# x first on SyncE's ring, all weights on ScalarE's, and sixteen small marks: a streamed x @ W kernel on one core

## Chip, cores and metric

One core of one Trainium2 chip. The metric is the device time of one execution in microseconds (us); the median of several. Each experiment is compared with runs of the kernel before on the same chip, beside it; a run over 1.5% above the fastest of its kernel is called slow and is left out of comparisons. Engines: TensorE (PE, its weight loads PEld), VectorE (DVE), ScalarE (ACT), GpSimd (POOL), SyncE (SP). "ACTq" and "SPq" in a profile are the queues of the two engines that issue DMAs here. I call what each feeds its ring; both rings run on the same 16 DMA engines.

## The reference

```python
W_adapted = W + scale * (lora_A @ lora_B)            # 256 x 256, rank 16
W_norm = np.sqrt(np.sum(W_adapted ** 2, axis=0, keepdims=True) + 1e-8)
W_final = W_adapted / W_norm * m
y = x.reshape(-1, 256) @ W_final                     # x: 32768 x 256, float32
```

32 MB of x come in, 32 MB of y go out; the weights are 256 KB of W, 16 KB each of lora_A and lora_B, 1 KB of m.

## The kernel before

x is cut into 8 blocks of 4 MB (128 rows of 32 KB, one per partition; the last block in two halves). There are five buffers. SyncE sends the first five loads at once; load b (b >= 5) waits until the store of block b - 5 has landed, since y overwrites x in the buffer and the buffer is then filled again.

```python
def load_x(n):
    nc.sync.dma_start(out=in_sbuf(*parts[n]), in_=in_dram(x_flat, *parts[n])
    ).then_inc(sem(f"load{n}"), 16)
def store_y(n):
    nc.scalar.dma_start(out=in_dram(out_flat, *parts[n]), in_=in_sbuf(*parts[n])
    ).then_inc(sem(f"store{n}"), 16)

nc.sync.dma_start(out=w_nat[:], in_=W...).then_inc(sem("load_w"), 16)
nc.scalar.dma_start(out=a_nat[:], in_=lora_A...).then_inc(sem("load_a"), 16)
nc.scalar.dma_start(out=b_nat[:], in_=lora_B).then_inc(sem("load_b"), 16)
nc.scalar.dma_start(out=m_row[:], in_=m[None, :]).then_inc(sem("load_m"), 16)
for n in range(len(parts)):
    b = parts[n][0] // CH
    if b >= XBUFS and parts[n][0] % CH == 0:
        nc.sync.wait_ge(sem(f"store{b - XBUFS}"), 16)
    load_x(n)
...
# VectorE, the end of the weights' chain
nc.vector.reciprocal(out=rnorm[:], in_=norm[:]).then_inc(dv, 1)
nc.vector.wait_ge(dv, 7)
for t in range(KC):
    i = nc.vector.tensor_mul(out=w_final[:, t], in0=wam[:, t], in1=rnorm[:])
i.then_inc(dv, 1)
...
# GpSimd: x to bf16 pairs, two chunks at a time, as soon as a block has landed
for p in range(NPR):
    ...
    nc.gpsimd.tensor_copy(out=xb_bufs[p % NXB][:], in_=x_bufs[...]).then_inc(sem("rounded"), 1)
...
# TensorE, in order: the weights' chain, then per pair of chunks transposes and products
nc.tensor.wait_ge(dv, 8)
...
# ScalarE: PSUM back into the x buffer; after each block drain(), then store_y(n)
```

Of the kernel before, what the change touches and what calls it, by code (L numbers as in the profile page):

```python
# [11 lines left out]
def kernel(  # L12
# [10 lines left out]
    nc = tc.nc  # L23
    P = 128
    FP32 = mybir.dt.float32
# [9 lines left out]
    KC = IN // P  # L35
# [7 lines left out]
    XBUFS = 5  # L43
    CH = DJ // J
# [15 lines left out]
    def sb(name, shape, dtype):  # L60
        return ctx.enter_context(nc.sbuf_tensor(name, shape, dtype))
# [7 lines left out]
    w_nat = sb("w_nat", [P, KC, OUT], FP32)  # L69
# [13 lines left out]
    norm = sb("norm", [P, OUT], FP32)  # L83
    rnorm = sb("rnorm", [P, OUT], FP32)
    m_all = sb("m_all", [P, OUT], FP32)
    w_final = sb("w_final", [P, KC, OUT], BF16)

    xt_ps = [ps(f"xt_ps{k}", [P, F8], FP32) for k in range(2)]
# [11 lines left out]
    def sem(name):  # L100
        if name not in sems:
            sems[name] = tc.alloc_semaphore(name)
        return sems[name]
# [4 lines left out]
    parts = [(b * CH, CH) for b in range(NBLK - 1)]  # L108
# [6 lines left out]
    def in_sbuf(g0, cnt):  # L115
        b, c = divmod(g0, CH)
        return x_bufs[b % XBUFS][:, c * J : (c + cnt) * J, :]

    def in_dram(dram, g0, cnt):
        return dram[g0 * J * P : (g0 + cnt) * J * P].rearrange("(p j) k -> p j k", p=P)  # L120

    def load_x(n):
        nc.sync.dma_start(
            out=in_sbuf(*parts[n]), in_=in_dram(x_flat, *parts[n])
        ).then_inc(sem(f"load{n}"), 16)

    def store_y(n):
# [2 lines left out]
        ).then_inc(sem(f"store{n}"), 16)  # L130


    nc.sync.dma_start(
        out=w_nat[:], in_=W.rearrange("(p t) o -> p t o", t=KC)
    ).then_inc(sem("load_w"), 16)
    nc.scalar.dma_start(
        out=a_nat[:], in_=lora_A.rearrange("(p t) r -> p t r", t=KC)
    ).then_inc(sem("load_a"), 16)
    nc.scalar.dma_start(out=b_nat[:], in_=lora_B).then_inc(sem("load_b"), 16)
    nc.scalar.dma_start(out=m_row[:], in_=m[None, :]).then_inc(sem("load_m"), 16)  # L140
    for n in range(len(parts)):
        b = parts[n][0] // CH
        if b >= XBUFS and parts[n][0] % CH == 0:
            nc.sync.wait_ge(sem(f"store{b - XBUFS}"), 16)
        load_x(n)


    nc.gpsimd.memset(zeros[:], 0.0).then_inc(sem("pool"), 1)
# [2 lines left out]
        out=identity[:],  # L151
        in_=zeros[:],
# [6 lines left out]
    for p in range(NPR):  # L159
        b, c = divmod(p, PRB)  # L160
        if p == 0 or part_of[2 * p - 1] != part_of[2 * p]:
            nc.gpsimd.wait_ge(sem(f"load{part_of[2 * p]}"), 16)
        if p >= NXB:
            nc.gpsimd.wait_ge(sem("turned"), p - NXB + 1)
        nc.gpsimd.tensor_copy(  # L165
            out=xb_bufs[p % NXB][:],
            in_=x_bufs[b % XBUFS][:, 2 * c * J : 2 * (c + 1) * J, :],
# [16 lines left out]
        out=wa[:], in0=ab_ps, scalar=float(scale), in1=w_nat[:], op0=ALU.mult, op1=ALU.add  # L184
# [15 lines left out]
    for p in range(NPR):  # L200
        nc.vector.wait_ge(sem("turned"), p + 1)
        nc.vector.tensor_copy(  # L202
            out=xt_bufs[p % NXT][:].rearrange("p r t -> p (r t)").bitcast(FP32),
            in_=xt_ps[p % 2][:],
# [8 lines left out]
        out=norm[:], in_=n2_ps, func=AF.Sqrt, bias=eps_col[:]  # L213
    ).then_inc(sem("act"), 1)
    for g in range(NCH):
        b, c = divmod(g, CH)
# [3 lines left out]
            out=x_bufs[b % XBUFS][:, c * J : (c + 1) * J, :], in_=y_ps[g % 2][:]  # L220
        ).then_inc(sem("room"), 1)
        n = part_of[g]
# [116 lines left out]
```

## Time and profile before

| | before |
|---|---|
| time, median of 3 runs | 163.86 us (163.66 to 163.94) |
| span of the profiled execution | 163.2 us (this run took 164.71; unprofiled runs of the same kernel beside e1 have spans of 162.1 to 162.6) |
| first store issued / sixth load may be sent (first store landed) | 34.5 us / 60.6 us |
| GpSimd's last wait for x ends; last store issued | 137.2 us; 148.2 us |

The profile's slices, the queues, SyncE's waits and the timeline of the start stand in the prediction. One more line of the groups matters later (count | busy us, mean ns of one | idle before): two multiplications of 128x256 took 2 us each, while another pair of the same shape (`wam`) took 0.42 us each.

```profile
L198 DVE TENSOR_TENSOR w_final<-wam,rnorm 128x256 bf16<-128x256 f32 x2 | 4.0, 2028 | 0.0
```

The trace also holds every DMA packet (its ring, size, start and duration, not its engine). Numbers called "packet records" come from there; their clock was set against the timeline by the landing of the first load, to about 0.1 us.

### The profile page before, as it was taken

Reading aid. Unit: us, or ns where it says so; the run is one execution under the profiler, and the core shown is the slowest. Engines: PE = TensorE matmul, PEld = TensorE weight load, DVE = VectorE, ACT = ScalarE, POOL = GpSimd, SP = SyncE. Lnnn points to the kernel's source line nnn. Section 1 sums busy time; section 2 is a strip of 40 time slices with the busy share of each in tenths; the row PEclk is TensorE's granted clock in tenths of the full one; section 3 lists DMA queues with packets and bytes.
Section 4 is the critical chain, followed back from the end, with each engine's and each line's share of the span. In section 5 each row is a group of like instructions: output and inputs, shape, how many; then the busy total and the mean of one; then the engine's idle time right before and its main releaser. Section 6 shows DMA issues by size and latency. Waiting matters only on the chain. (4 is left out here: it accounts for less than half of the span.)

```text
span 163.2 us, 1988 instructions
## 1 busy us (share of the span) xinstructions
PE 105.3 (65%) x786; PEld 85.2 (52%) x786; DVE 47.2 (29%) x44; ACT 63.8 (39%) x67; POOL 62.5 (38%) x39
## 2 busy tenths in 40 slices
PE   1270599789789897898981998619988820892000
PEld 0130577677577775776760867418676610771000
DVE  0429452350532514405230325005051400330000
ACT  3010027548366384473754053900738440062000
POOL 1006381753935738268004940069209003900000
PEclk9999999999999999999998589985899996599755
DMA  5998998998999999999999999999999999998991
GB/s 201 402 498 386 426 474 385 482 418 265 466 426 426 442 410 466 426 394 482 418 426 442 420 426 458 402 458 410 446 414 454 414 446 422 450 442 377 442 430 60
DMA packets 2915, 67.41 MB, mean 413 GB/s; under 512 B 465, under 2 KB 482, under 8 KB 610
## 3 DMA queue, kind: packets, MB, share of 16 engines
q1 hardware_dynamic: 1440, 33.82, 49.0%
q10 hardware_dynamic: 1474, 33.59, 47.8%
q14 instruction: 1, 0.01, 0.0%
HBM read 33.85 MB, written 33.55 MB: 413 GB/s over the span
## 5 line engine op out<-in xcount | busy, mean ns | idle before, releaser
L219 ACT COPY x_sb<-y_ps 128x1024 f32<-128x1024 f32 x64 | 61.9, 1014 | 75.8 <-PE y_ps L281 75.8
L165 POOL CAST xb<-x_sb 128x2048 bf16<-128x2048 f32 x32 | 60.0, 1902 | 79.3 <-DMA x_sb<-in_x_dram 56.0
L281 PE MATMUL y_ps<-w_final,xt 128*128 128x256 bf16 x512 | 64.6, 280 | 12.8 <-PEq L256 12.8
L202 DVE COPY xt<-xt_ps 128x1024 f32<-128x1024 f32 x32 | 38.2, 1221 | 88.1 <-PE xt_ps L267 88.0
L281 PEld LDWEIGHTS y_ps<-w_final,xt 128*128 128x128 bf16 x512 | 48.4, 100 | 28.2 <-issue 19.8
L267 PE MATMUL xt_ps<-identity,xb 128*128 128x128 f32 x264 | 39.1, 309 | 23.1 <-PEq L256 23.1
L267 PEld LDWEIGHTS xt_ps<-identity,xb 128*128 128x128 f32 x264 | 34.9, 161 | 25.8 <-issue 25.6
L198 DVE TENSOR_TENSOR w_final<-wam,rnorm 128x256 bf16<-128x256 f32 x2 | 4.0, 2028 | 0.0
L244 PE MATMUL y_ps<-sq,ones 128*128 128x256 f32 x4 | 2.1, 674 | 1.6 <-DVE sq L187 1.6
L233 PE MATMUL y_ps<-identity,a_nat 128*16 128x128 f32 x2 | 0.6, 397 | 3.6 <-DMA a_nat<-in_lora_A_dram 3.6
L212 ACT ACTIVATE norm<-y_ps,eps_col 128x256 f32<-128x256 f32 x1 | 0.5, 473 | 6.1 <-PE y_ps L244 6.1
L244 PEld LDWEIGHTS y_ps<-sq,ones 128*128 128x128 f32 x4 | 1.2, 323 | 2.3 <-DVE sq L187 2.1
L210 ACT ACT_TABLE_LOAD x1 | 1.3, 1283 | 2.4 <-issue 2.4
L233 PEld LDWEIGHTS y_ps<-identity,a_nat 128*16 128x16 f32 x2 | 0.1, 90 | 3.6 <-issue 3.6
L171 POOL MEMSET xb<- 128x2048 bf16 x1 | 1.8, 1805 | 0.3 <-PE xt_ps L267 0.3
L195 DVE RECIPROCAL rnorm<-norm 128x256 f32<-128x256 f32 x1 | 1.7, 1745 | 0.0
L237 PE MATMUL y_ps<-b_bf,aT 16*128 16x256 bf16 x2 | 0.6, 404 | 1.5 <-DVE aT L180 1.5
L189 DVE COPY m_all<-y_ps 128x256 f32<-128x256 f32 x1 | 0.4, 425 | 3.3 <-PE y_ps L249 3.3
L178 DVE CAST b_bf<-b_nat 16x256 bf16<-16x256 f32 x1 | 0.3, 281 | 3.8 <-DMA b_nat<-in_lora_B_dram 3.8
L249 PE MATMUL y_ps<-m_row,ones 1*128 1x256 f32 x2 | 1.2, 710 | 0.0
L237 PEld LDWEIGHTS y_ps<-b_bf,aT 16*128 16x128 bf16 x2 | 0.1, 106 | 1.9 <-DVE aT L180 1.9
L183 DVE SCALAR_TENSOR_TENSOR wa<-y_ps,w_nat 128x512 f32<-128x512 f32 x1 | 0.7, 692 | 0.8 <-PE y_ps L237 0.8
(13 smaller groups left out, 3.7 us busy)
## 6 DMA issues: line engine op xcount, KB each, us to landing
x_sb<-in_x_dram SPq DMA_DIRECT2D x7, 4096.0 KB, 27.1
out_dram<-x_sb ACTq DMA_DIRECT2D x7, 4096.0 KB, 37.2
x_sb<-in_x_dram SPq DMA_DIRECT2D x2, 2048.0 KB, 29.6
out_dram<-x_sb ACTq DMA_DIRECT2D x2, 2048.0 KB, 20.2
w_nat<-in_W_dram SPq DMA_DIRECT2D x1, 256.0 KB, 2.9
a_nat<-in_lora_A_dram ACTq DMA_DIRECT2D x1, 16.0 KB, 2.6
b_nat<-in_lora_B_dram ACTq DMA_DIRECT2D x1, 16.0 KB, 3.6
m_row<-in_m_dram ACTq DMA_DIRECT2D x1, 1.0 KB
```

The costliest lines, as they stand in the source:

```text
L165: nc.gpsimd.tensor_copy(out=xb_bufs[p % NXB][:], in_=x_bufs[b % XBUFS][:, 2 * c * J : 2 * (c + 1) * J, :],).then_inc(sem("rounded"), 1)
L171: nc.gpsimd.memset(xb_bufs[NPR % NXB][:], 0.0).then_inc(sem("rounded"), 1)
L183: nc.vector.scalar_tensor_tensor(out=wa[:], in0=ab_ps, scalar=float(scale), in1=w_nat[:], op0=ALU.mult, op1=ALU.add).then_inc(dv, 1)
L195: nc.vector.reciprocal(out=rnorm[:], in_=norm[:]).then_inc(dv, 1)
L198: i = nc.vector.tensor_mul(out=w_final[:, t], in0=wam[:, t], in1=rnorm[:])
L202: nc.vector.tensor_copy(out=xt_bufs[p % NXT][:].rearrange("p r t -> p (r t)").bitcast(FP32), in_=xt_ps[p % 2][:],).then_inc(sem("copied"), 1)
L210: nc.scalar.activation(out=warm[:], in_=eps_col[:], func=AF.Sqrt)
L219: nc.scalar.copy(out=x_bufs[b % XBUFS][:, c * J : (c + 1) * J, :], in_=y_ps[g % 2][:]).then_inc(sem("room"), 1)
L244: i = nc.tensor.matmul(n2_ps, ones[:], sq[:, t, :], start=(t == 0), stop=(t == KC - 1))
L249: nc.tensor.matmul(mb_ps, ones[0:1, :], m_row[:], start=True, stop=True).then_inc(pe, 1)
L267: i = nc.tensor.transpose(xt_ps[p % 2][:, j * P : (j + 1) * P], xb_bufs[p % NXB][:, j, :].bitcast(FP32), identity[:],)
L281: i = nc.tensor.matmul(y_ps[h][:, j, :], xt_bufs[p % NXT][:, r : r + P, t], w_final[:, t, :], start=(t == 0 and (j % (J // 2)) == 0), stop ...
```

## The change

Intent: x, the long stream, should not stand behind W; so all weights go to ScalarE's ring. Sixteen loads of 1 to 16 rows, with row lengths of 68 to 128 bytes, are put behind the fifth load so that they can be told apart in the trace.

```diff
-    nc.sync.dma_start(
-        out=w_nat[:], in_=W.rearrange("(p t) o -> p t o", t=KC)
-    ).then_inc(sem("load_w"), 16)
     nc.scalar.dma_start(out=a_nat[:], ...
+    nc.scalar.dma_start(
+        out=w_nat[:], in_=W.rearrange("(p t) o -> p t o", t=KC)
+    ).then_inc(sem("load_w"), 16)
     nc.scalar.dma_start(out=b_nat[:], ...
     nc.scalar.dma_start(out=m_row[:], ...
     for n in range(len(parts)):
         b = parts[n][0] // CH
+        if b == XBUFS and parts[n][0] % CH == 0:
+            for k in range(1, 17):
+                nc.sync.dma_start(
+                    out=marks[0:k, k, 0 : 16 + k], in_=lora_B[0:k, 0 : 16 + k]
+                ).then_inc(sem("marks"), 16)
         if b >= XBUFS and parts[n][0] % CH == 0:
             nc.sync.wait_ge(sem(f"store{b - XBUFS}"), 16)
         load_x(n)
+    nc.sync.wait_ge(sem("marks"), 256)
```

More of the change, by code (lines that the diff above doesn't have):

```diff
@@ L85 @@
     m_all = sb("m_all", [P, OUT], FP32)
+    marks = sb("marks", [16, 17, 32], FP32)
     w_final = sb("w_final", [P, KC, OUT], BF16)
```

## The prediction

> **What bounds the kernel now.** I read the slices of the span first, then the queues, then the waits, then the timeline of the start.
>
> ```profile
> DMA  5998998998999999999999999999999999998991
> GB/s 201 402 498 386 426 474 385 482 418 265 466 426 426 442 410 466 426 394 482 418 426 442 420 426 458 402 458 410 446 414 454 414 446 422 450 442 377 442 430 60
> ...
> q1 hardware_dynamic: 1440, 33.82, 49.0%
> q10 hardware_dynamic: 1474, 33.59, 47.8%
> HBM read 33.85 MB, written 33.55 MB: 413 GB/s over the span
> ```
>
> The DMA engines are busy in every slice; the two rings (q1 is SyncE's, q10 ScalarE's) together take 96.8% of 16 engines' span. No compute engine passes 65%, and the chain of work that ended last is only 145 to 148 us: what follows is stores draining. So the time is one start (first packet at 2.45 us) plus the packets of 67.4 MB plus whatever the DMA engines stand idle. In the trace's packet records each 4 MB load or store is 128 rows of 32 KB, 8 per DMA engine, and the median row takes 1.213 us on either ring; 8 blocks in and out are 128 rows per engine, 128 x 1.213 = 155.3 us. With the start and some 2 us of small packets and stalls, most engines end near 160 us; one ends at 163.2. Only something that makes DMA engines idle can cost much here, and only removed idle time can gain.
>
> ```profile
> SPq L123 <- DMA out_dram<-x_sb: 95.5, 3, 56.8
> ...
> POOL xb L165 <- DMA x_sb<-in_x_dram: 56.0, 6, 12.2
> ```
>
> There are five buffers: SyncE sends five loads at once, then waits 56.8 us for the first store to land before it may send the sixth. Until then the SyncE ring holds 40 rows per engine, 40 x 1.213 = 48.5 us of work, and no more. If the stores start after these have run out, nothing is left to move. When they start is set by the weights:
>
> ```profile
> 0.90 0.40 ACTq L136 DMA_DIRECT2D a_nat<-in_lora_A_dram  x1
> 0.94 0.37 SPq L133 DMA_DIRECT2D w_nat<-in_W_dram  x1
> ...
> 1.33 0.45 ACTq L139 DMA_DIRECT2D b_nat<-in_lora_B_dram  x1
> 1.36 2.39 SPq L123 DMA_DIRECT2D x_sb<-in_x_dram  x5
> ...
> 5.00 0.28 DVE L178 CAST b_bf<-b_nat 16x256 bf16<-16x256 f32 x1 [3.79 <-DMA b_nat<-in_lora_B_dram]
> ...
> 14.05 3.98 DVE L198 TENSOR_TENSOR w_final<-wam,rnorm 128x256 bf16<-128x256 f32 x2
> 18.30 3.27 PEld L267 LDWEIGHTS xt_ps<-identity,xb 128*128 128x128 f32 x16 [7.92 <-issue]
> ...
> 34.52 0.37 ACTq L128 DMA_DIRECT2D out_dram<-x_sb  x1
> ```
>
> lora_B lands at 4.95 us, the chain from it to w_final ends at 18.03, TensorE only then begins on x (in order), and the first store is issued at 34.52: 29.6 us after lora_B. Later stores follow each 13.2 us (47.74, 60.96, 74.22, 87.43), less than the 2 x 9.7 us that a block's load and store take, so compute has slack. With five loads sent at 1.4 us the loads alone would end near 52 us; the first store comes 18 us before that. This slack hides the weights today.
>
> **What the Trainium skill says.** "DMA: Bandwidth & Descriptors", section "Issuing engines are not separate DMA queues": DMAs of all issuers end on the same 16 engines and interleave. The trace agrees: both rings are busy together at an unchanged sum near 430 GB/s. Same page, "Queues, rings and completion order": an engine round-robins between rings and drains a whole packet, typically 9 to 17 descriptors, before it switches. The trace fits a turn of one descriptor better. m's single 1 KB row came at 6.30 us and its semaphore write at 7.55, one 32 KB row between them. And from 3.2 to 3.5 us, while lora_A (8 rows of 128 bytes per engine) and W (8 of 2 KB) were both in the rings, 40 packets of the one and 52 of the other started, mixed; lora_A packets went on until 3.5 us, which a whole group of 8 at 13 ns each would not. Same page, "Why a DMA increments its semaphore by 16 and not by 1": k of the 16 engines take part, the lowest-numbered, with k from the outer sizes. The trace shows one data packet for m and 16 for lora_B. So of marks with 1 to 16 rows, engine 0 gets 16 and engine 15 one.
>
> **The change part by part.** Compute is untouched but for line numbers; the comparison of the two orders moves only DMA issues.
>
> (a) x goes first on SyncE's ring: W's issue (0.42 us) leaves the way, and its 8 x 84 ns = 0.67 us per engine are moved, not saved. DMA starts at 2.45 us either way. Gain: none, as bytes bind.
>
> (b) The weights all stand on ScalarE's ring, against x rows of 1.213 us instead of each other. Per engine: lora_A 8 packets and a semaphore write, W 8 and one, lora_B one and one: 20 turns. Before, in the first 0.1 us of packets 27 of lora_A's 128 had started and 5 of W's, so the slowest engine gets perhaps one or none out ahead: 19 to 20 turns, each behind one record of SyncE's ring. 19 to 20 such records are 17 or 18 rows and 2 semaphore writes. 17.5 x 1.213 = 21.2, plus W's 0.67, plus a first row that takes some 0.3 longer (1.35 to 1.69 us in the trace), after 2.5: lora_B lands at 24.7 us, 19.7 later than now. W lands about one row earlier, m two turns later, in time for its matmul 4.9 us after lora_B.
>
> (c) The first store moves from 34.52 to 34.52 + 19.7 = 54.2 us. The five loads end at 2.5 + 0.3 + 48.6 + 0.8 (weights) = 52.2. The DMA engines then stand. Before, the first store's rows came 5.55 us after its issue (40.07), of which up to 1.2 was a running x row, and x rows were slowed to 2 to 2.9 us meanwhile (the slice of 265 GB/s; 1.5 us lost per engine). I take 3.0 us from issue to flow: 1.5 as at the start of the kernel (issue at 0.94, packet at 2.45) and this 1.5. Flow at 57.2, so 5.0 us idle.
>
> (d) The first store alone takes 9.7 us, to 66.9; the second is issued at 54.2 + 13.2 = 67.4 and flows at 68.9; the sixth load, sent on the first store's landing, flows at 66.9 + 1.5 = 68.4. Idle 1.5 us. After that ten blocks are left, 97 us, with a load and a store in hand at each step: block 4 is computed to 107 us, load 5 lands near 88. Nothing starves.
>
> (e) The marks: 16 data and 16 semaphore packets on engine 0, 2 on engine 15, near 10 ns each. They come after the fifth load, when by (c) the other ring is empty: under 1 us, in idle time. SyncE's issue of 16 x 0.4 us ends at 10 us while its ring is full.
>
> Sum: 5.0 + 1.5 idle, less the 1.5 us that the stall cost before and that (c) counts again, = +5.0. 163.86 + 5.0 = 168.9 us.
>
> **Rivals.** First: turns are whole packets, as the skill says. Then lora_B takes 6 turns, lands near 10 us, the first store goes at 39.6, 12 us before the loads run out: no idle, 163.5 to 164.3. For it: the page; against: m and the mixture above.
>
> Second, following from the first: if stores flow when the marks come up, each of engine 0's 32 mark packets waits behind a 1.21 us store row, up to 39 us, and the sixth load on engine 0 lands near 105 instead of 86.5. Compute then stalls at block 5. But the engine moves stores meanwhile, and the last store would be issued near 150 with backlog left: 163.5 to 168.
>
> Third: the slack of compute vanishes. TensorE would run without the pauses of 8 to 11 us that it has now from 88 us on; the granted clock already falls to 0.84 in 90 to 110 us. If blocks then take 16 us, the last store is issued near 157, still under the 166 at which the rows end; slower yet gives up to 172.
>
> Fourth: the author's hope, x first by 0.4 us and all else hidden: 163.4.
>
> **Range and chances.** Turns of one descriptor I hold to be 80% likely; then 165.5 to 171.5, as lora_B's landing and the store's start-up each are good to 1.5 us and count one for one. Otherwise near 164. Range 163.6 to 171.5. The line of 2% is 167.14, 1.8 us under my figure: slower 0.70, same 0.27, faster 0.03.
>
> **What would show it.** lora_B landing at 23 to 26 us (about 10 in the first rival); w_final ending near 37.7; first store issued at 53 to 56; one or two slices of low GB/s between 52 and 70 us; SyncE's first wait for a store longer than 56.8 us by some 8; no pause of GpSimd for x at the sixth block; the total bytes unchanged. Wrong if the slices stay at 9 throughout, or if the sixth load lands late on engine 0 alone. If lora_B is late as said and the time still within 2%, then the idle gap was mis-sized: the store's start-up of 3 us or the 17.5 rows.

## The result

The changed kernel takes 165.63 us in the median (165.49, 165.62, 165.64, and one slow run of 169.02); the kernel before, beside it, 163.9. The ratio is 1.0104 (95% interval 1.0085 to 1.0124). Ratios here are the mean time of one kernel's fast runs over that of the other's of the same rounds, so not quite the ratio of the medians. The forecast was +5.0 us; measured is +1.7, a third of it.

The slices of the changed kernel, to set beside those in the prediction: no slice of low DMA share between 52 and 70 us, where I had expected the engines to stand.

```profile
DMA  5999999999999899999989999999999999999992
GB/s 187 457 408 416 428 472 392 472 424 392 488 400 384 384 472 370 384 440 448 384 384 464 432 400 480 402 428 412 444 444 436 408 476 400 464 424 400 428 444 88
```

The timeline of the changed kernel (start us, duration, engine and line; in brackets the idle time before and who ended it):

```profile
0.90 0.40 ACTq L135 DMA_DIRECT2D a_nat<-in_lora_A_dram  x1
0.94 2.66 SPq L124 DMA_DIRECT2D x_sb<-in_x_dram  x5
...
1.33 0.45 ACTq L138 DMA_DIRECT2D w_nat<-in_W_dram  x1
1.81 0.45 ACTq L141 DMA_DIRECT2D b_nat<-in_lora_B_dram  x1
...
13.75 3.73 POOL L174 CAST xb<-x_sb 128x2048 bf16<-128x2048 f32 x2 [12.07 <-DMA x_sb<-in_x_dram]
21.54 0.28 DVE L187 CAST b_bf<-b_nat 16x256 bf16<-16x256 f32 x1 [20.32 <-DMA b_nat<-in_lora_B_dram]
...
30.59 0.76 DVE L207 TENSOR_TENSOR w_final<-wam,rnorm 128x256 bf16<-128x256 f32 x2
31.62 3.28 PEld L276 LDWEIGHTS xt_ps<-identity,xb 128*128 128x128 f32 x16 [4.71 <-issue]
...
47.37 0.37 ACTq L129 DMA_DIRECT2D out_dram<-x_sb  x1
...
63.36 39.38 SPq L124 DMA_DIRECT2D x_sb<-in_x_dram  x4
```

lora_B is there at 21.5 us (4.95 before; 24.7 forecast). W lands 17.6 us after its issue instead of 2.9. The two multiplications to w_final take 0.76 us together instead of 3.98; GpSimd's first casts are long over (e12 and other runs below show that this is the reason). The first store is issued at 47.37 us: 12.9 later than before, not 19.7. SyncE waits 53.1 us for it. That is less than the 56.8 of before only because the issues of the marks keep SyncE busy until 10.3 us, so that the wait begins later; the store lands at 63.3 us, 2.8 later than before (60.55):

```profile
SPq L124 <- DMA out_dram<-x_sb: 90.9, 3, 53.1
```

In the packet records the first store's rows flow from 51.8 us and the last row of the five loads ends at 54.6. The rows of the store came 2.8 us before the loads ran out, so the DMA engines never stood. But SyncE's ring, which before always had the sixth load queued behind the fifth, was without x rows from 54.6 to 68.0 us: 8.7 us until the store had landed, and 4.6 more from the issue of the sixth load (63.36) to its first row. (The sixth load of before began no earlier, at 68.4, but behind the fifth without a break.) The records differ in their slow rows. Summing over all rows what each took beyond 1.213 us (0.611 for a row of 16 KB), per DMA engine:

| stretch, us | before | changed |
|---|---|---|
| 0 to 5 (first rows of x) | 0.1 | 0.6 |
| 34 to 55 (first store's start) | 1.3 | 0.7 |
| 55 to 70 (sixth load's and second store's start) | 0.0 | 0.8 |
| 70 to 90 (third store's start) | 0.0 | 0.6 |
| whole execution | 1.65 | 2.95 |
| landing of the last store's 16 parts: mean, latest | 160.4, 163.2 | 161.5, 163.9 |

So 1.3 us more of DMA time per engine are lost in rows that take 1.4 to 2.4 us instead of 1.2: 0.5 more in the first 5 us, 0.6 less at the first store, 1.4 more between 55 and 90 us. The first part goes with x first, not with the gap: the kernels below that send x first in whole blocks have 0.5 to 0.7 us there, with a gap or without, those with W first 0.1. The later slow rows are mostly rows of the other ring in the last 1 to 5 us before a ring's rows begin again: SyncE's at 49 to 52 us, before the first store's rows (51.8); ScalarE's at 62 to 68, before the sixth load's (68.0); SyncE's at 76 to 81, around the start of the third store's (79.7). (The profiled run of before was 0.8 us slower than its neighbours. Two later kernels with the same start and typical spans of 162.2 us, e4 and e5 below, have 1.1 to 1.2 us of slow rows, and their last stores land at 159.8 and 160.1 in the mean, 162.2 and 162.1 at the latest; against them the changed kernel has 1.8 us more of slow rows and ends 1.4 to 1.7 us later in the mean, 1.7 to 1.8 at the latest, which is about the measured difference.)

### The profile page after: what moved, and what is told of

Same layout as the page of the kernel before. It is cut to its first block, busy times and chain, and to the rows that moved or that the text cites. A ratio compares the mean times of both kernels' runs of the same rounds, so it can differ in the third digit from the quotient of the medians.

```text
span 164.0 us, 2005 instructions
## 1 busy us (share of the span) xinstructions
PE 99.6 (61%) x786; PEld 81.5 (50%) x786; DVE 43.8 (27%) x44; ACT 63.6 (39%) x67; POOL 62.3 (38%) x39
## 3 DMA queue, kind: packets, MB, share of 16 engines
q10 hardware_dynamic: 1618, 33.85, 48.5%
## 5 line engine op out<-in xcount | busy, mean ns | idle before, releaser
L228 ACT COPY x_sb<-y_ps 128x1024 f32<-128x1024 f32 x64 | 61.7, 1014 | 60.8 <-PE y_ps L290 60.8
L290 PE MATMUL y_ps<-w_final,xt 128*128 128x256 bf16 x512 | 62.7, 275 | 14.1 <-PEq L265 14.1
L290 PEld LDWEIGHTS y_ps<-w_final,xt 128*128 128x128 bf16 x512 | 47.4, 98 | 28.6 <-issue 21.0
L276 PE MATMUL xt_ps<-identity,xb 128*128 128x128 f32 x264 | 35.4, 291 | 12.4 <-PEq L265 12.4
L276 PEld LDWEIGHTS xt_ps<-identity,xb 128*128 128x128 f32 x264 | 32.2, 151 | 14.0 <-issue 13.8
L258 PEld LDWEIGHTS y_ps<-m_row,ones 1*128 1x128 f32 x2 | 0.5, 308 | 0.7 <-issue 0.7
## 6 DMA issues: line engine op xcount, KB each, us to landing
w_nat<-in_W_dram ACTq DMA_DIRECT2D x1, 256.0 KB, 17.6
b_nat<-in_lora_B_dram ACTq DMA_DIRECT2D x1, 16.0 KB, 19.7
```

The costliest lines, as they stand in the source:

```text
L228: nc.scalar.copy(out=x_bufs[b % XBUFS][:, c * J : (c + 1) * J, :], in_=y_ps[g % 2][:]).then_inc(sem("room"), 1)
L258: nc.tensor.matmul(mb_ps, ones[0:1, :], m_row[:], start=True, stop=True).then_inc(pe, 1)
L276: i = nc.tensor.transpose(xt_ps[p % 2][:, j * P : (j + 1) * P], xb_bufs[p % NXB][:, j, :].bitcast(FP32), identity[:],)
L290: i = nc.tensor.matmul(y_ps[h][:, j, :], xt_bufs[p % NXT][:, r : r + P, t], w_final[:, t, :], start=(t == 0 and (j % (J // 2)) == 0), stop ...
```

## The experiments

Two theories after the result. A: the late weights leave SyncE's ring empty, because the sixth load must wait for a late first store; bytes flow on, but each new start costs slow rows. B: the marks cost the time, by turns against store rows. A third thing had to be checked: whether the terms of my sum were as I read them (one turn per descriptor; the idle gap if the store is late enough; the cast beside the multiplications).

**e1: no marks.**

```diff
 (changed kernel)
-        if b == XBUFS and ...: sixteen mark loads
-    nc.sync.wait_ge(sem("marks"), 256)
```

> The changed kernel without its sixteen marks. Theory A (late weights make rings run empty, and each new start of a ring costs the DMA engines 0.6 to 0.8 us): nothing changes, 165.4 to 165.8 us, lora_B lands near 21.5 us, first store issued near 47.4. Theory B (the marks cost the time, by turns against store rows): back to 163.7 to 164.2 us.

Measured: runs of 164.46, 165.25 (fast), and 167.24, 167.49, 167.71, 168.35 (slow); before beside it 163.7. The reported verdict is unclear (ratio 1.0194, which is more than the two fast runs by themselves give: their mean is 1.007 times the 163.7). The profiled fast run has lora_B at 21.5, 3.0 us of slow rows and a mean landing of the last store's parts at 161.5, as in the changed kernel, but its latest part lands at 163.1 instead of 163.9. So without the marks the slow rows and the late end are still there: B as the whole cause is refuted in the trace. The times are too scattered to give the fast part better than +0.8 to +1.6 us, and do not exclude that the marks cost some tenths. Why two thirds of the runs fell in a slower state, I have no profile to say; their granted clocks (0.941 to 0.944) lie between those of the two fast runs (0.932 and 0.950).

**e2: marks only.** The kernel before, with the sixteen mark loads and the wait for them.

```diff
 (kernel before)
+        if b == XBUFS and ...: sixteen mark loads
+    nc.sync.wait_ge(sem("marks"), 256)
```

> The kernel before plus the sixteen marks, weights as before. Theory A: 163.7 to 164.4 us; the marks come up while stores flow (from 67 us), take a turn against a 1.21 us row each, and the sixth load lands late (100 to 107 us instead of 87.7) on the engines with most marks, but bytes still bind. Theory B: 165 us or more.

Measured: fast runs 167.65, 167.94, 168.90, ratio 1.0286 (1.0253 to 1.0318), slower. My theory A expected no cost and missed; B's figure came true in a kernel in which B's cause really acts. GpSimd's timeline and the slices:

```profile
113.78 3.73 POOL L173 CAST xb<-x_sb 128x2048 bf16<-128x2048 f32 x2 [35.85 <-DMA x_sb<-in_x_dram]
```

```profile
DMA  5999989899999999999999999999999799098997
GB/s 197 450 434 403 482 379 497 387 387 371 450 418 418 450 411 466 419 435 419 403 466 419 444 426 403 426 415 454 422 415 430 336 387 497 8 505 379 399 422 316
```

The sixth block arrives at 113.8 us instead of 87.8. This is the second rival of the prediction: the marks come up at 68 us while stores flow. In the packet records the 16 rows of the last mark (128 bytes) start one after another at 68.5, 71.0, 72.8, 75.2, 77.8 ... 99.9, 104.2: an engine with one mark more takes 2.4 us more in the mean (104.2 - 68.5, over 15), two turns (data and semaphore write) of one store row each. The one with all sixteen begins the sixth load near 106 us instead of 69. Compute starves, the stores run out, and the DMA engines stand, most of all in the slice of digit 0 and 8 GB/s (141 to 145 us): 4.4 us idle per engine in all. I had written that bytes would still bind; they did not. In the changed kernel the same marks began to take turns at 55 us, but the first store had been alone on the other ring and ended at 62.7; the remaining marks all passed between 62.7 and 63.5. The late weights protected it.

**e3: W in two loads**, nine turns more on ScalarE's ring.

```diff
 (changed kernel)
-    nc.scalar.dma_start(out=w_nat[:], in_=W...)
+    for t in range(KC):
+        nc.scalar.dma_start(out=w_nat[:, t, :], in_=W...[:, t, :]).then_inc(sem("load_w"), 16)
...
-nc.vector.wait_ge(sem("load_w"), 16)
+nc.vector.wait_ge(sem("load_w"), 32)
```

> The changed kernel with W loaded as two DMAs of 8 rows of 1 KB per engine instead of one of 8 rows of 2 KB: 9 more turns on the ring of ScalarE (8 rows and a semaphore write). If a turn is one descriptor: lora_B lands 9 x 1.21 = 10.9 us later, at 32.4, first store issued at 58.3 us, after the five loads have ended (near 55); the DMA engines then stand still for 4 to 7 us and the time is 169 to 172 us. If turns go by packets of many descriptors: lora_B at most 2.5 us later and the time unchanged at 165.6.

Measured: 172.98 us (172.95 to 173.04), ratio 1.0563. Timeline and windows of this kernel (in the windows the last two columns are DMA share and GB/s):

```profile
31.20 0.28 DVE L188 CAST b_bf<-b_nat 16x256 bf16<-16x256 f32 x1 [29.99 <-DMA b_nat<-in_lora_B_dram]
...
57.48 0.37 ACTq L129 DMA_DIRECT2D out_dram<-x_sb  x1
```

```profile
48.00:53.00 5.00, 4.31 (x40) 3.76 (x38) 2.36 (x2) 2.47 (x3) 2.27 (x2) 1.00 0.77 318
53.00:58.00 5.00, 4.68 (x42) 3.90 (x40) 0.76 (x1) 3.86 (x4) 2.20 (x2) 1.00 0.00 0
58.00:63.00 5.00, 4.00 (x36) 3.25 (x36) 1.59 (x2) 2.87 (x4) 3.00 (x2) 1.00 0.98 419
...
68.00:73.00 5.00, 4.32 (x40) 3.76 (x39) 2.36 (x2) 2.29 (x3) 2.51 (x2) 1.00 0.76 256
```

9.7 us later for nine turns of 1.21 us, one of which fell to a semaphore write: a turn is one descriptor. And the gap that I had predicted for the changed kernel is here, with both its parts: 5.7 us from the loads' end (53.1) to the first store row (58.8), and a second one near 68 to 70. Idle time per engine is 7.4 us. So a first store later than the loads in hand does make the engines stand, as forecast; the changed kernel was on the near side of that edge. (That each microsecond beyond it costs one is not shown by this one run.) On idle engines the store flowed 1.3 us after its issue; beside running loads it took 4.4 us in the changed kernel and 5.5 before.

**e4: the cast held until w_final is done.**

```diff
 (kernel before)
+        if p == 0:
+            nc.gpsimd.wait_ge(sem("dve"), 8)
```

> The kernel before with GpSimd's first cast held until w_final is done. If GpSimd's cast slowed VectorE's two multiplications to w_final (2028 ns each before, 0.38 us each in the changed kernel, where no cast ran beside them), they take 0.38 us here too, w_final is done at 14.8 us, the first transpose begins at about 16.9 instead of 18.3, the first store is issued 1.4 us earlier at 33.1, and the time stays 163.6 to 164.2 since bytes bind. If the cast is not the reason they stay near 2 us.

Measured: 163.66 us, ratio 0.9992 (0.9972 to 1.0011). The multiplications took 0.38 us each (half of the pair's time; the profile's mean for one is 421 ns, as the two overlap) and the first store went at 32.72. But lora_B landed at 4.1 us in this run, 0.9 earlier than in the profile of before, so w_final (done at 13.9 us) would have been done by the time of the first cast anyway: it says nothing about the cast. Nor does it say what an earlier first store is worth: e5, which does not hold the cast, also sent its first store at 32.5, so the unprofiled runs of before may have done so too.

**e5: a trickle on ScalarE's ring** until the first store.

```diff
 (kernel before, after the load of m)
+    for k in range(3):
+        nc.scalar.dma_start(out=trickle[:, k, :], in_=lora_A[0:P, :]).then_inc(sem("trickle"), 16)
```

> The kernel before plus three tiny loads on the ring of ScalarE behind m: 8 packets of 64 bytes and a semaphore write per engine each, 27 turns of 1.21 us, so that this ring is not empty when the first store comes at 34.5 us. If the slow rows of 36 to 41 us (1.2 us per engine over 1.213 a row) are the price of a ring that starts from empty, they shrink to under 0.4 us and the time falls to 162.5 to 163.1. If they are the price of the first store itself, they stay and the time is 163.5 to 164.

Measured: 163.87 us beside 163.81, ratio 1.0010. The slow rows at the first store stay (0.85 us per engine; 0.83 in e4). So an empty ring by itself does not make the first store dear; that part of theory A falls.

**e6: x first, W second on the same ring**, no marks.

```diff
 (kernel before)
-    nc.sync.dma_start(out=w_nat[:], ...)
...
         load_x(n)
+        if n == 0:
+            nc.sync.dma_start(out=w_nat[:], ...)
```

> x first on SyncE's ring, W second on the same ring behind the first 4 MB, the three small weights on ScalarE's ring, no marks. W lands near 13 us, lora_B near 10.5; w_final near 22, first store near 38 us, 14 us before the five loads end. If the cost of the change comes from late weights that let the rings run empty: none here, 163.5 to 164.1 us. If x ahead of the weights costs by itself: 164.5 or more.

Measured: 164.14 us (163.74 to 164.84), ratio 1.0020 (1.0002 to 1.0037). The time is at the upper edge of the first case, but its premise was wrong: the first store went at 39.65, landed after the five loads had ended (61.8), and SyncE's ring had no x row until 68.1. The profiled run was the slowest of the six (164.84), with 2.85 us of slow rows; how many the faster ones had is not known. Small cost, with slow rows at the same places. In passing, the groups show the cast's effect: `sq` has the same shape and takes 691 to 693 ns in all kernels but this one, where GpSimd's first cast (13.65 to 17.84 us) ran beside it.

```profile
L188 DVE TENSOR_TENSOR sq<-wa 128x512 f32<-128x512 f32 x1 | 1.3, 1266 | 0.0
```

**e7: blocks 0 and 5 in halves** (weights and x as in the changed kernel, no marks).

```diff
-    parts = [(b * CH, CH) for b in range(NBLK - 1)] + two halves of the last
+    parts: blocks 0, 5 and 7 in halves, the others whole; the sixth load's
+    halves each wait for the store of the half block whose buffer they fill
```

> The changed kernel without marks, and with blocks 0 and 5 loaded and stored in halves, whose rows are 16 KB (0.61 us a turn instead of 1.21). All 15 turns of the weights fall in the first block: if a turn lasts as long as the row that the other ring has there, lora_B lands near 12 to 13 us instead of 21.5, the first half store goes near 32 us, no ring runs empty before 60 us, and the time is 163.5 to 164.2. If not, lora_B stays near 21 us.

Measured: 163.59 us (163.55 to 163.82) beside 163.81, ratio 0.9994. Timeline:

```profile
13.50 0.28 DVE L186 CAST b_bf<-b_nat 16x256 bf16<-16x256 f32 x1 [12.29 <-DMA b_nat<-in_lora_B_dram]
...
32.89 0.37 ACTq L133 DMA_DIRECT2D out_dram<-x_sb  x1
```

A turn lasts as long as the row that the other ring has there: 0.61 us, and lora_B comes 8 us sooner. SyncE's ring never ran empty (loads end 61.6, the sixth flows from 61.7), slow rows are down to 0.87 us, and the cost of the change is gone.

**e8: the first store in halves, first load whole**, so that the weights stay late.

```diff
 (e1)
+    block 0 is stored in two halves (rows of 16 KB); block 5 is loaded in two halves,
+    each waiting for one of the two stores
```

> The changed kernel without marks; block 0 loaded whole but stored in two halves, the sixth load in two halves that each wait for one. The weights come as late as in the changed kernel (lora_B 21.5). The first half store goes 6.6 us earlier, near 40.8 us, so the ring of ScalarE is running before the loads end and the sixth load can be sent near 55 us instead of 64. If empty rings are the cost: 164.0 to 164.8 us, between before (163.7) and the changed kernel without marks. If late weights cost by something else: no change from that kernel (164.5 to 167).

Measured: 164.32 us (164.06 to 164.86), ratio 1.0034 (1.0019 to 1.0049): between, as theory A had it, with SyncE's ring without rows for 6.1 us (56.7 to 62.8) instead of 14.9. The slow rows hardly shrank (2.7 us against 3.0), but here too the profiled run was the slowest; and at 0.5 us over before its runs overlap with the fast ones of e1 (164.46 and 165.25, on another chip). It points to A and does not prove it.

**e10: quarters.** (A version with a sixth buffer, which would have been the plain test, was not run; that it does not fit in SBUF is my count and not a run.)

```diff
 (e1)
+    block 0 stored in four quarters; blocks 4 and 5 loaded in quarters,
+    each quarter of block 5 waiting for one of the four stores
```

> The changed kernel without marks; block 0 is stored in quarters, the fifth and sixth block are loaded in quarters, each quarter of the sixth waiting for one of the stores. The weights stay as late as in the changed kernel (lora_B near 21.5 us, w_final near 31.3), but the first quarter store goes near 39 us and lands near 50, before the loads in hand have ended (near 58), so the ring of SyncE never runs empty. If the empty ring is the cost: rows slower than 1.213 us add up to under 1.6 us per engine (2.95 in the changed kernel) and the time is 163.5 to 164.1. If late weights or x first cost by themselves: 164.5 or more.

Measured: 164.68 to 167.06 in five fast runs, ratio 1.0120 (1.0072 to 1.0168). A miss. SyncE's ring did not run empty and the slow rows at 55 to 90 us did go (under 0.1 us against 1.4). But rows of 8 KB took 309 ns, so 1.236 us per 32 KB instead of 1.213, which makes 0.6 us of the slow rows counted in the table below; others came at other places (0.7 us at the first store, 0.8 after 90 us). And one DMA engine fell behind: the semaphore writes of the later loads come 15 together and one 2 to 7 us after, and compute waited for that one. The test that was to settle theory A brought a new wait with it: by its slow rows at 55 to 90 us A holds, by its time nothing is settled, and that late weights cost something by themselves is not excluded.

**e11: the kernel before, with blocks 0 and 5 in halves**, the attempt at a version that beats both.

```diff
 (kernel before)
-    parts: only block 7 in halves
+    parts: blocks 0, 5 and 7 in halves, with the waits of e7
```

> The kernel before (W first on SyncE's ring) with blocks 0 and 5 in halves, as in the run with halves: an attempt at a version that beats both. The first store's slow rows (1.3 us per engine before) should shrink to 0.2 as they did there (0.15), and with them the time to 162.5 to 163.2; if the bytes and the one late engine at the end set it alone, 163.4 to 163.9.

Measured: 163.48 us (163.44 to 163.89) beside 163.85, ratio 0.9977 (0.9956 to 0.9997). The first store's slow rows shrank to about 0.6 us (25 to 40 us; this store's rows begin at 29.6), not to 0.2, and 0.7 came back after 90 us. The fastest of all, by 0.2%, which is the second of the two expected cases. In passing, the first half block came at 9.4 us, so that GpSimd's first casts (9.45 to 13.4 us) fell beside the multiplications to `wam`, which take 0.42 us each elsewhere:

```profile
L199 DVE TENSOR_TENSOR wam<-wa,m_all 128x256 f32<-128x256 f32 x2 | 2.5, 1304 | 0.0
```

**e12: the cast on purpose beside w_final.**

```diff
 (e1)
+        if p == 0:
+            nc.gpsimd.wait_ge(sem("dve"), 7)
```

> The changed kernel without marks, with GpSimd's first two casts held until rnorm is ready, so that they run beside the two multiplications to w_final, as in the kernel before. If GpSimd's cast is what made those two take 2028 ns each there, they take about 2 us each here instead of 0.38, the first store is issued 3.2 us later, at 50.6 us instead of 47.4 to 48.2, and the time grows by 0 to 1.5 us, as the first store then flows about when the loads end. If not, they stay at 0.38 us and the store at 48 to 49.5.

Measured: 165.30 us (165.06 to 165.69), ratio 1.0086.

```profile
30.32 2.45 DVE L201 TENSOR_TENSOR w_final<-wam,rnorm 128x256 bf16<-128x256 f32 x2
30.35 4.17 POOL L168 CAST xb<-x_sb 128x2048 bf16<-128x2048 f32 x2 [28.67 <-DVE rnorm L198]
```

The first multiplication began 0.03 us before the cast and took 0.43 us; the second began beside it and took 2.11 (2.45 us for both, against 0.76 alone and 3.98 in the kernel before, where both began after a cast and took 1.95 and 2.10); the casts grew from 3.73 to 4.17. The effect is real, half as large as I had put it, since here VectorE began first. TensorE began on x at 33.07 us (31.59 in e1), the store was issued at 48.5 (48.2 in e1; 50.6 was expected); against e1's two fast runs the time cannot be told apart.

All kernels in one table. "Gap" is from the last row of the five loads in hand to the first row of the sixth (about 1.3 us is one row of the other ring, so no gap); "slow rows" as above, per DMA engine; both from the profiled run. Where block 0 is stored in parts, the first part counts.

| kernel | first store issued | gap on SyncE's ring | slow rows | of these at 55 to 90 us | fast runs, us |
|---|---|---|---|---|---|
| before | 34.5 | 1.3 | 1.65 | 0.0 | 163.4 to 164.4 |
| e4 | 32.7 | 1.6 | 1.1 | 0.0 | 163.4 to 163.8 |
| e5 trickle | 32.5 | 1.1 | 1.2 | 0.0 | 163.6 to 164.2 |
| e7 halves | 32.9 | 0.1 | 0.9 | 0.1 | 163.6 to 163.8 |
| e11 | 25.2 | 0.6 | 1.6 | 0.1 | 163.4 to 163.9 |
| e8 | 41.1 | 6.1 | 2.7 | 1.5 | 164.1 to 164.9 |
| e6 | 39.7 | 6.3 | 2.85 | 1.6 | 163.7 to 164.8 |
| changed | 47.4 | 13.4 | 2.95 | 1.4 | 165.5 to 165.6 |
| e1 no marks | 48.2 | 14.9 | 3.0 | 1.8 | 164.5 to 165.3 |
| e12 | 48.5 | 15.2 | 2.75 | 1.7 | 165.1 to 165.7 |
| e3 | 57.5 | 17.2 | 3.05, and 7.4 idle | 1.6 | 173.0 |
| e10 | 39.2 | none | 2.8 | 0.1 | 164.7 to 167.1 |
| e2 marks only | 34.7 | 4.1, and up to 39 on one engine | 2.0, and 4.4 idle | 0.1 | 167.7 to 168.9 |

Without a gap, slow rows stay under 1.7 us and the time near 163.7; with a gap of 6 us or more they are 2.7 to 3.05, and the time is 0.3 to 1.8 us longer (e3, whose engines also stood, apart). e10 is the exception, for the reasons above. The column for 55 to 90 us has none: 1.4 to 1.8 us with a gap of 6 us or more, at most 0.1 below that, in e10 and e2 too. The size of the cost is less clear than its place: e6, e8 and the changed kernel have nearly the same slow rows in their profiled runs and cost 0.3, 0.5 and 1.7 us in the median.

## Why the prediction was wrong

The mechanism of the main step was right; two terms of its sum were too large, and together they crossed an edge beyond which the sum no longer applied. The step that failed is (c): "The DMA engines then stand". With the first store at 47.4 us instead of 54.2 they did not. That 165.63 us still lies within the 165.5 to 171.5 given for turns of one descriptor is luck: the idle time on which that range was built is not in it.

1. *Turns of one descriptor* (b): right. In the packet records of the changed kernel lora_A's last packets start in sets of 16, one per engine, at 4.2 to 4.9, 5.5 to 6.1 and 6.7 to 7.3 us, its semaphore writes at 7.9 to 8.6, and W's eight per engine from 9.1 to 17.6. e3 and e7 confirm it by count and by row length.
2. *"the slowest engine gets perhaps one or none out ahead: 19 to 20 turns"* (b): wrong. Five of eight lora_A packets per engine (79 or 80 of 128) started by 3.4 us, before or beside the first x row, which took until 4.2 to 4.9 us (the records do not tell engines apart). 15 turns were left, and lora_B landed at 21.5 us instead of 24.7. I had read 27 packets in the first 0.1 us of the kernel before as all of the head start; here such packets went on starting for 1 us.
3. *The chain of 29.6 us from lora_B to the first store* (used in (c)): wrong. It took 25.8. Of the 3.8 us, 3.2 are the two multiplications to w_final: 2 x (2028 - 422) ns. Before, GpSimd's casts ran beside them; with late weights the casts had ended 13 us before (17.5 and 30.6 us). I carried over a duration that belonged to a coincidence of the old timing. e12, `wam` in e11 and `sq` in e6 show the effect. The Trainium skill has it, and I had not looked it up: "SBUF — State Buffer", section "SBUF: two separate sides", says that a VectorE operation with two SBUF inputs and a GpSimd operation that reads SBUF lock each other out for a whole instruction. The trace agrees: 2028 ns instead of 422 for w_final, 1266 instead of 692 for `sq`, while `wa`, with one input in PSUM, took 694 ns also in e6, beside the cast.
4. So the first store came at 47.4, not 54.2 (c), and its rows at 51.8, before the loads' end. The loads ended at 54.6 rather than 52.2; in e3, where no store ran beside them, they ended at 53.1, so 1.5 us of this are from sharing the last stretch with the store. The *3.0 us from issue to flow* were too few as well (4.4 beside running loads); the forecast had named this start-up and the 17.5 rows as its weak terms, but not the chain. The *idle of 5.0 + 1.5 us* did not come; e3 shows that it does come with a first store at 57.5.
5. What came in its place is +1.7 us of another kind, which (c) had only as a one-time 1.5: slow rows around the new start of rings after SyncE's ring had been without x rows (1.4 us at 55 to 90 us), and some at the start of x (0.5). I had even subtracted it (and recounted, the stall of before is 1.3). The table supports that the gap brings the rows at 55 to 90 us, and e7, with earlier weights and no gap, shows no cost. e5 has slow rows at the first store although small packets kept its ring filled, so an empty ring alone is not the mechanism. What the DMA engines do in those rows, and how much of the 1.7 us each place costs, stays open.
6. *Marks* (e): right as far as the runs tell, since no cost of theirs stands clear of the noise here (e12 without them takes 165.1 to 165.7, with them it was 165.5 to 165.6). But the reason is not the one I gave: they did not come in idle time but took turns against the first store, until it ended at 62.7. The second rival, for which I gave 163.5 to 168, was true of the marks without the late weights (e2), and its statement that backlog would be left was not.
7. *x first gains nothing* (a): right; the first x block was there for GpSimd's cast at 13.75 us, and at 13.83 before.
8. The third rival did not show: the granted clock was 0.93 against 0.91, and compute kept its slack: GpSimd still waited for x 5.0, 6.3 and 10.8 us from 103 us on. (The *pauses of 8 to 11 us* that the prediction gives TensorE are misread: such pauses are GpSimd's, 7 to 12 us; TensorE's own are 3.5 to 7.5.)

## What to carry to other kernels

A small load on one ring beside long rows on the other waits one row per descriptor, semaphore writes included (here 1.21 us, and 0.61 beside rows of half the length); let what starts the chain go out before the stream begins (in the kernel before, with W ahead of x, lora_B was there at 4.95 us), or make the rows beside it short. When work moves in time, check for each duration that is carried over what ran beside it in the old profile. And when a predicted cost depends on one time passing another, name the distance to that edge: in the forecast it was 5.0 us, less than the 7.0 us by which the two terms (3.2 and 3.8) were off.

## What the Trainium skill lacked or had wrong

- "DMA: Bandwidth & Descriptors", "Queues, rings and completion order": it has an engine drain a packet of typically 9 to 17 descriptors per turn. For these loads a turn was one descriptor: one lora_A packet per engine for each 32 KB row, nine turns for eight rows and a semaphore write (9.7 us, e3), two turns per mark in e2.
- Same page, "Issuing engines are not separate DMA queues": that a second issuer only saves issue time leaves out that the choice of ring sets when a small load lands: W landed 17.6 us after its issue beside x, 2.9 us ahead of it.
- No page has the slow rows around a ring's new start, mostly on the other ring before it: 1.4 to 2.9 us instead of 1.213 for some 4 us, 0.2 to 1.3 us per DMA engine and occasion. Nor has one the time from issue to first row beside a running ring, 3.9 to 5.7 us for the first stores here against 1.3 on idle engines, or that five small packets per engine got out before or beside the first row of a stream (the changed kernel).
